# DeltaNet values in a hybrid decoder trunk: convolution along the partitions with shifted copies through DRAM, in place of transposes on TensorE

## The chip, the cores and the metric

The kernel runs on one core of one Trainium2 chip. The metric is the device time of one execution in microseconds (us); the time before is the median of three runs. The profile is one further execution, with its own time. TensorE is called PE (PEld is its weight load), VectorE DVE, ScalarE ACT, GpSimd POOL and SyncE SP. SP computes nothing here; it issues transfers (DMAs), as ACT does too.

## The reference, cut to what matters

There are 256 tokens of width 2048 and two layers. Each layer normalises, projects to 8208 columns, mixes in two branches, projects back, and adds a gated embedding. The change touches the values v of the DeltaNet branch, which has 8 heads of 128:

```
def causal_conv(x, w):      # CONV_WIDTH = 4, one filter per column
    return lax.conv_general_dilated(x, w[:, None, :], (1,), [(CONV_WIDTH - 1, 0)], ...)

def deltanet_branch(qkv, z, b, a, conv_w, A_log, dt_bias, norm_w):
    qkv = jax.nn.silu(causal_conv(qkv, conv_w))
    q, k, v = jnp.split(qkv, 3, axis=-1)
    ...
    o = chunk_gated_delta_rule(q, k, v, g, beta)
    return gated_head_norm(o, z, norm_w)
```

So a value column at token t is silu of the sum over j = 0 to 3 of w[3 - j] times the projected column at token t - j, with zeros ahead of token 0. All is float32.

## The kernel before, in words

The three large products (`in`, `out`, `gate`) run as 392 steps of weights, mostly 512 KB each. For each step SP loads a `raw` tile (`load`, L351), ACT copies it rounded into `whi` (`prep`, L366), DVE makes the remainder `wlo` = raw - whi (L368), and PE multiplies 2 token halves by `whi` and `wlo` (L309): three matmuls for each of two (or four) blocks of 128 rows. There are 3 buffers each of `raw`, `whi` and `wlo`; `ahead` loads up to 4 steps ahead and prepares up to 2 ahead. A step of 12 such matmuls of 512 columns takes some 2.7 us.

The mixers are Python generators that a `tick` after each step advances. A generator yields a count of ticks, out of the tables `DELAY` and `DELAY_AT` (`d2t64`: DeltaNet group 2, step t64), or a condition. A group g has two heads, so 4 groups in 2 layers make 8 instances; `dn12` is layer 1, group 2. Matmuls and transposes go to PE in the order of the program. The other instructions are ordered by a scheduler that works with estimated times, and then each engine runs its own list strictly in that order. SP and ACT issue DMAs the same way: an instruction that waits holds what stands behind it in its own list.

For v (`DN.dv`) the projection comes out of PE with the tokens on the partitions. `evict` (L544) copies it from PSUM to an `et` tile with the row scale, on ACT. After one tick `turned` transposes it on PE (4 transposes of 128x128, `pvc`, L312), so that the columns lie on the partitions and the tokens along a row. `conv` multiplies by the last filter tap on ACT (2 instructions, L607), then adds the other three taps on DVE with slices shifted along the row (6 scalar_tensor_tensor, L611). `sigmoid` takes three ACT and one DVE instructions (L411 to L418), and a DVE product makes silu (L780). After `v` ticks (5; 6 in groups 0 and 3) it is transposed back (4 transposes, `pv`), and DVE scales it by `invn` into `R` (L787). `R` is read much later, when the triangular solve of the group is done.

That solve has a part of its own on DVE, in `q_side` after the wait F: 15 pairs of a product (L701) and a sum (L704) of a small 32-row tile, each needing the one before. It already uses DRAM to rearrange: `d1` is written and read, then `d2`, all issued by ACT.

Buffers that matter: `tmp` has 6 tiles of 128x512, `et` has 2 tiles of 128x1024 shared with the q, k and HGRN2 evictions, and PSUM has 5 banks for the mixers.

Of the kernel before, what the change touches and what calls it, by code (L numbers as in the profile page):

```python
# [16 lines left out]
NG = 4  # L17
# [8 lines left out]
def chunk_cols(chunk):  # L26
# [3 lines left out]


DELAY = {
    "d": {'c': 1, 'D': 4, 'k': 5, 'q': 5, 'ssq': 1, 'F': 3, 'T': 9, 't16': 2, 'p16': 2, 't32': 2, 'p32': 2, 't64': 2, 'p64': 2, 'v': 5, 'z0': 1, 'S': 1, 'w': 1, 'z1': 1, 'o': 1, 'y': 3, 'yp': 1},
    "b": {'o': 1, 'g': 4},
    "h": {'c': 1, 'f': 1, 'a': 4, 'u1': 3, 'u4': 3, 'u16': 3, 'o': 2, 'y': 2, 'yp': 1, 'q': 0},
}

DELAY_AT = {
# [9 lines left out]
}  # L48
# [105 lines left out]


@with_exitstack
def trunk(ctx: ExitStack, tc: tile.TileContext, head, xT, x, pT, W, par, fw, cst, msk, eye, out):
    nc = tc.nc
    pool = lambda name, bufs, **kw: ctx.enter_context(tc.tile_pool(name=name, bufs=bufs, **kw))
    cp = pool("const", 1)  # L160
# [92 lines left out]

    dr = pool("scratch", 1, space=bass.MemoryType.DRAM)
    d2 = dr.tile([66048], F32, name="d2")
    dfull = lambda d: d.rearrange("(i x) -> i x", i=4)[:, 0:16384].rearrange("i (p c) -> p i c", c=128)
    ddiag = lambda d: d.rearrange("(q x) -> q x", q=32)[:, 0:2048].rearrange("q (s f) -> q s f", s=16)[:, :, 0:16]
    SLr = cp.tile([128, 128], F32R, name="SLr")
# [3 lines left out]
    def clear_scratch():  # L262
        V.tensor_copy(SLr, SL)
        G.memset(hA[64:128, :, 0:64], 0.0)
        zero = tp.tile([128, 512], F32, tag="tmp", name="zero")
        G.memset(zero, 0.0)
        tc.keep_in_program_order(nc.scalar.dma_start(out=dfull(d2), in_=zero.rearrange("p (i c) -> p i c", i=4)))

    def P(name, i, n=1):
        o = PAR[name][0] + i  # L270
# [240 lines left out]
    def mix(tag, n, bufs, name):  # L511
        return mp.tile([128, n], F32, tag=tag, name=name, bufs=bufs)

    def v4(ap):
        return ap.rearrange("p (a b) -> p a b", b=128)
# [24 lines left out]
    def evict(ps, c0, n, rt, name):  # L540

        et = mix("et", 1024, 2, name + "et")[:, :2 * n].rearrange("p (t n) -> p t n", t=2)
        for t in range(2):
            S.activation(et[:, t], ps[t][:, c0:c0 + n], AF.Copy, scale=rt[:, t:t + 1])  # L544
        return et

    def turned(et, c0, name):

        ps = pm.tile([128, 512], F32, tag="m", name=name)
        for i in range(4):  # L550
            hh, t = divmod(i, 2)
            PE.transpose(ps[:, 128 * i:128 * i + 128], et[:, t, c0 + 128 * hh:c0 + 128 * hh + 128], ident)
        return ps
# [5 lines left out]
    class DN:  # L559
# [214 lines left out]

        def dv(self, ps, c0):
            n, kq, g = self.n, self.kq, self.g
            et = evict(ps, c0, 256, self.row.rt, n + "v")
            yield self.wait("c")
            ac, sg = self.conv(turned(et, 0, n + "pvc"), 2)
            V.tensor_tensor(ac, ac, sg, ALU.mult)  # L780
            yield self.wait("v")
            yield self.after("k")
            pv = pm.tile([128, 512], F32, tag="m", name=n + "pv")
            for i in range(4):
                PE.transpose(pv[:, 128 * i:128 * i + 128], ac[:, 128 * i:128 * i + 128], ident)
            R = v4(mix("R", 512, 2, n + "R"))
            V.tensor_tensor(R, v4(pv), bc(self.invn, 128), ALU.mult)  # L787
            yield self.after("T")
            yield self.wait("z0")
            v1 = v4(mix("v1", 512, 1, n + "v1"))  # L790

            pz = pm.tile([128, 512], F32, tag="m", name=n + "pz0")
            for hh in range(2):
                PE.matmul(pz[:, 128 * hh:128 * hh + 128], self.Tt[:, 2 * hh], R[:, 2 * hh], start=True, stop=True)
            V.tensor_tensor(v1[:, 0::2], v4(pz)[:, 0:2], bc(self.b[:, 0::2], 128), ALU.mult)
            yield self.wait("S")
            pS = pm.tile([128, 512], F32, tag="m", name=n + "pS")
            for hh in range(2):
                PE.matmul(pS[:, 128 * hh:128 * hh + 128], v4(self.ktail)[:, hh], v1[:, 2 * hh], start=True, stop=True)
            St = v4(mix("St", 256, 1, n + "St"))  # L800
            S.copy(St, v4(pS)[:, 0:2])
            yield self.wait("w")

            pw = pm.tile([128, 512], F32, tag="m", name=n + "pw")
            for hh in range(2):
                for w in range(2):
                    PE.matmul(pw[:, 256 * hh + 128 * w:256 * hh + 128 * w + 128], kq[:, hh, 1, w, :], St[:, hh],
                              start=True, stop=True)
            for hh in range(2):
                V.scalar_tensor_tensor(R[:, 2 * hh + 1], pw[:, 256 * hh:256 * hh + 128], self.neG[:, hh:hh + 1],  # L810
                                       R[:, 2 * hh + 1], ALU.mult, ALU.add)
            qs = v4(mix("qs", 256, 1, n + "qs"))
            V.tensor_tensor(qs, v4(pw)[:, 1::2], bc(self.eG, 128), ALU.mult)
            yield self.wait("z1")
            pz = pm.tile([128, 512], F32, tag="m", name=n + "pz1")
            for hh in range(2):
                PE.matmul(pz[:, 128 * hh:128 * hh + 128], self.Tt[:, 2 * hh + 1], R[:, 2 * hh + 1], start=True, stop=True)
            V.tensor_tensor(v1[:, 1::2], v4(pz)[:, 0:2], bc(self.b[:, 1::2], 128), ALU.mult)
            yield self.wait("o")
            po = pm.tile([128, 512], F32, tag="m", name=n + "po")  # L820
            for i in range(4):
                PE.matmul(po[:, 128 * i:128 * i + 128], self.QK[:, i], v1[:, i], start=True, stop=True)
            o = v4(tmp(n + "o"))
            S.copy(o[:, 0::2], v4(po)[:, 0::2])
            V.tensor_tensor(o[:, 1::2], v4(po)[:, 1::2], qs, ALU.add)
            ss = small("sso")
            for i in range(4):
                S.activation(sp.tile([128, 128], F32, tag="junk", name="junk", bufs=1), o[:, i], AF.Square,
                             scale=self.nq[:, i:i + 1], accum_out=ss[:, i:i + 1])
            f = small("fo")  # L830
            rms_factor(f, ss)
            V.tensor_tensor(f, f, self.nq, ALU.mult)
            yield self.wait("y")
            yield self.after("z")
            yield from head_norm(o, f, self.sz, P("dnw", self.l), g, self.y, n, self.wait("yp"))
# [445 lines left out]
```

## Time and profile before

| | |
|---|---|
| median of three runs (range) | 1279.0 us (1278.23 to 1279.3) |
| the profiled execution: its time / its span | 1276.74 / 1275.0 us |
| granted PE clock, mean | 0.997 |
| PE busy | 1257.1 us (99%) |
| DVE busy | 924.9 us (73%) |
| ACT busy | 782.8 us (61%) |
| POOL busy | 64.0 us (5%) |
| chain that ended last | PE 93%, DVE 5%, issue 1%, ACT 1% |
| DMA | 220.88 MB, SP's queue 51.0% of 16 engines' time, ACT's 2.2% |

The span runs from the first to the last instruction; the profiled execution took 1.74 us more than its span. A busy share says how long an engine had work, not whether it could have done the work faster. Durations of PE overlap: how long a matmul holds PE is read from one start to the next.

### The profile page before, as it was taken

To read this page: it belongs to the slowest core of one execution; us is meant where nothing else is said; L and a number is where in the kernel's file an instruction comes from. 1 tells how busy PE (TensorE), PEld (TensorE's weight loads), DVE (VectorE), ACT (ScalarE), POOL (GpSimd) and SP (SyncE) were. 2 spreads that over 40 slices of the span, in tenths; PEclk is the share of its full clock that TensorE was granted. 3 is DMA by queue.
4 is the path that set the end of the run, shared out by engine and by line. 5 is a ranking of instruction groups with operands and counts; after the bars stand their busy time and mean duration, and the time that the engine had idled before them with its cause. 6 is when DMAs were issued, how large, how long until landed. Compare 5 with 4: busy or idle time off the path is not lost.

```text
span 1275.0 us, 19572 instructions
## 1 busy us (share of the span) xinstructions
PE 1257.1 (99%) x7240; PEld 1044.4 (82%) x7240; DVE 924.9 (73%) x1736; ACT 782.8 (61%) x1400; POOL 64.0 (5%) x55
## 2 busy tenths in 40 slices
PE   8999999999999999999999999999999999999996
PEld 7988887888887888888888888888888888888885
DVE  7789679787796855547668886897777968565575
ACT  7666666666666654437557667667666766444464
POOL 0100010020000000000002000100100000000010
PEclk9999999999999999999999999999999999999998
DMA  8565545445554455555555545544555545555563
GB/s 276 187 226 175 165 153 166 141 158 182 161 173 150 148 172 179 186 187 192 183 186 167 179 163 156 169 145 131 179 180 172 159 149 178 178 182 182 182 198 132
DMA packets 78753, 220.88 MB, mean 173 GB/s; under 512 B 15553, under 2 KB 25281, under 8 KB 78657
## 3 DMA queue, kind: packets, MB, share of 16 engines
q1 hardware_dynamic: 59840, 212.14, 51.0%
q10 hardware_dynamic: 18816, 7.48, 2.2%
q8 instruction: 57, 0.93, 0.3%
q14 instruction: 40, 0.32, 0.1%
HBM read 214.88 MB, written 4.72 MB: 172 GB/s over the span
## 4 chain that ended last, share of the span: by engine, by line
PE 93%; DVE 5%; issue 1%; ACT 1%; DMA 0%; SPq 0%; DVEq 0%; ACTq 0%
PE out L309 14%; PE gate L309 14%; PE in0dk L309 7%; PE in1dk L309 7%; PE in1hf L309 6%; PE in0hf L309 6%; PE in0dv L309 6%; PE in1dv L309 6%; PE in0hi L309 5%; PE in1hi L309 5%; PE up L309 2%; DVE wlo L368 1%; PE in0dz L309 1%; PE in1dz L309 1%; DVE dn12pr L701 0%
## 5 line engine op out<-in xcount | busy, mean ns | idle before, releaser
L368 DVE TENSOR_TENSOR wlo<-raw,whi 128x1024 fp32r<-128x1024 f32 (+1 forms) x394 | 482.4, 1227 | 253.6 <-ACT whi L366 251.6
L366 ACT ACTIVATE whi<-raw 128x1024 fp32r<-128x1024 f32 (+1 forms) x394 | 413.4, 1051 | 356.7 <-PE out L309 88.3
L309 PE MATMUL in1hf<-whi,n1hi 128*128 128x512 f32 x128 | 52.5, 410 | 0.0
L309 PE MATMUL in1hi<-whi,n1hi 128*128 128x512 f32 x128 | 51.6, 403 | 0.0
L309 PE MATMUL in1dk<-whi,n1hi 128*128 128x512 f32 x128 | 51.2, 400 | 0.0
L309 PE MATMUL in1dk<-wlo,n1hi 128*128 128x512 f32 x128 | 50.1, 392 | 0.2 <-DVE wlo L368 0.2
L309 PE MATMUL gate<-whi,g0hi 128*128 128x512 f32 x128 | 50.2, 392 | 0.0
L309 PE MATMUL in1hf<-whi,n1lo 128*128 128x512 f32 x128 | 50.1, 391 | 0.0
L309 PE MATMUL in1hi<-whi,n1lo 128*128 128x512 f32 x128 | 50.0, 391 | 0.0
L309 PE MATMUL in1dk<-whi,n1lo 128*128 128x512 f32 x128 | 50.0, 390 | 0.0
L309 PE MATMUL in1hf<-wlo,n1hi 128*128 128x512 f32 x128 | 49.9, 390 | 0.0
L309 PE MATMUL gate<-whi,g1hi 128*128 128x512 f32 x128 | 49.9, 390 | 0.0
L309 PE MATMUL in1hi<-wlo,n1hi 128*128 128x512 f32 x128 | 49.9, 390 | 0.0
L309 PE MATMUL gate<-whi,g0lo 128*128 128x512 f32 x128 | 49.8, 389 | 0.0
L309 PE MATMUL gate<-wlo,g0hi 128*128 128x512 f32 x128 | 49.8, 389 | 0.0
L309 PE MATMUL gate<-wlo,g1hi 128*128 128x512 f32 x128 | 49.8, 389 | 0.0
L309 PE MATMUL gate<-whi,g1lo 128*128 128x512 f32 x128 | 49.8, 389 | 0.0
L309 PE MATMUL in1dv<-whi,n1hi 128*128 128x512 f32 (+1 forms) x128 | 48.4, 378 | 0.0
L309 PE MATMUL in1dv<-wlo,n1hi 128*128 128x512 f32 (+1 forms) x128 | 46.6, 364 | 0.0
L309 PE MATMUL in1dv<-whi,n1lo 128*128 128x512 f32 (+1 forms) x128 | 46.6, 364 | 0.0
L309 PE MATMUL in0hf<-whi,n0hi 128*128 128x512 f32 x96 | 39.2, 408 | 0.0
L309 PE MATMUL in0hi<-whi,n0hi 128*128 128x512 f32 x96 | 38.5, 401 | 0.0
(1549 smaller groups left out, 3229.0 us busy)
## 6 DMA issues: line engine op xcount, KB each, us to landing
raw<-W SPq DMA_DIRECT2D x384, 512.0 KB, 3.5
raw<-W SPq DMA_DIRECT2D x7, 544.0 KB, 4.1
h<-x SPq DMA_DIRECT2D x4, 512.0 KB, 5.2
xt<-xT SPq DMA_DIRECT2D x3, 512.0 KB, 7.4
out_dram<-h SPq DMA_DIRECT2D x6, 256.0 KB, 2.1
fw<-fw ACTq DMA_DIRECT2D x2, 512.0 KB, 6.0
pin<-pT ACTq DMA_DIRECT2D x2, 256.0 KB, 3.3
out_dram<-h ACTq DMA_DIRECT2D x2, 256.0 KB, 3.0
```

What stands on the lines that cost most here:

```text
L309: return tc.keep_in_program_order(nc.tensor.matmul(*a, **k))
L366: S.activation(hi[:, sl], raw[:, sl], AF.Copy)
L368: V.tensor_tensor(lo[:, sl], raw[:, sl], hi[:, sl].bitcast(F32), ALU.subtract)
```

## The change

The tokens stay on the partitions. `dv` evicts v as before into one half of an `et` tile, and ACT writes it (256 KB) into a DRAM scratch `dsh` behind three rows of zeros. One tick later (`vl`) SP loads the group's filter, repeated on 128 partitions (`cvw`, a new input; 512 KB), and three copies of v, shifted by 1, 2 and 3 tokens (256 KB each). Three ticks later (`vc`) DVE multiplies the four copies by the four rows of the filter and adds them up; the sigmoid follows. After `v` (now 2) ticks four scalar_tensor_tensor write R = conv x invn x sigmoid. Neither `pvc` nor `pv` is transposed any more; the two PSUM banks for them go. At the start two small DMAs on ACT's queue clear the rows of zeros. The delays of a few other steps are changed too.

```diff
-    "d": {... 't64': 2, 'p64': 2, 'v': 5, 'z0': 1, ...},
+    "d": {... 't64': 2, 'p64': 2, 'vl': 1, 'vc': 3, 'v': 2, 'z0': 1, ...},
...
-    "d0D": 6, "d0k": 6, "d0p16": 4, "d0p32": 3, "d0p64": 1, "d0q": 7, "d0t64": 3, "d0v": 6,
+    "d0D": 6, "d0k": 6, "d0p16": 4, "d0p32": 3, "d0p64": 1, "d0q": 7, "d0t64": 3,
...
-    "d2D": 9, "d2k": 3, "d2t64": 4, "d2y": 4, "d2yp": 2, "d2z1": 2,
-    "d3k": 6, "d3o": 2, "d3p64": 3, "d3v": 6, "d3w": 2,
-    "h0a": 5, "h0yp": 2,
-    "h1f": 2, "h1u4": 4, "h1yp": 3,
+    "d2D": 9, "d2k": 3, "d2t16": 1, "d2t64": 6, "d2y": 4, "d2yp": 2,
+    "d3k": 6, "d3o": 2, "d3p64": 3, "d3w": 2,
+    "h0a": 5, "h0u1": 2, "h0yp": 2,
+    "h1f": 2, "h1u4": 4, "h1y": 1, "h1yp": 3,
...
+    dsh = [dr.tile([256 * 259], F32, name=f"dsh{j}") for j in range(2)]
...
+        for d in dsh:
+            tc.keep_in_program_order(nc.scalar.dma_start(out=d[0:768].rearrange("(p f) -> p f", p=128), in_=zero[:, 0:6]))
...
         def dv(self, ps, c0):
             n, kq, g = self.n, self.kq, self.g
-            et = evict(ps, c0, 256, self.row.rt, n + "v")
-            yield self.wait("c")
-            ac, sg = self.conv(turned(et, 0, n + "pvc"), 2)
-            V.tensor_tensor(ac, ac, sg, ALU.mult)
+            full = mix("et", 1024, 2, n + "vet")
+            et, x1 = full[:, :512], full[:, 512:]
+            d = dsh[g % 2]
+            for t in range(2):
+                sl = slice(256 * t, 256 * t + 256)
+                S.activation(et[:, sl], ps[t][:, c0:c0 + 256], AF.Copy, scale=self.row.rt[:, t:t + 1])
+            v2 = lambda ap: ap.rearrange("p (t n) -> p t n", t=2)
+            rows = lambda j: d[256 * (3 - j):256 * (259 - j)].rearrange("(t p n) -> p t n", t=2, p=128)
+            nc.scalar.dma_start(out=rows(0), in_=v2(et))
+            wv = mix("cvw", 1024, 1, n + "cvw")
+            yield self.wait("vl")
+            nc.sync.dma_start(out=wv, in_=cvw[self.l * NG + g])
+            xs = [x1, tmp(n + "vs2"), tmp(n + "vs3")]
+            for j, x in enumerate(xs, 1):
+                nc.sync.dma_start(out=v2(x), in_=rows(j))
+            yield self.wait("vc")
+            w = lambda j: bc1(wv[:, 256 * j:256 * j + 256], 2)
+            V.tensor_tensor(v2(et), v2(et), w(3), ALU.mult)
+            for j, x in enumerate(xs, 1):
+                V.tensor_tensor(v2(x), v2(x), w(3 - j), ALU.mult)
+                V.tensor_tensor(et, et, x, ALU.add)
+            sigmoid(x1, et)
             yield self.wait("v")
             yield self.after("k")
-            pv = pm.tile([128, 512], F32, tag="m", name=n + "pv")
-            for i in range(4):
-                PE.transpose(pv[:, 128 * i:128 * i + 128], ac[:, 128 * i:128 * i + 128], ident)
             R = v4(mix("R", 512, 2, n + "R"))
-            V.tensor_tensor(R, v4(pv), bc(self.invn, 128), ALU.mult)
+            for i in range(4):
+                hh, t = divmod(i, 2)
+                sl = slice(256 * t + 128 * hh, 256 * t + 128 * hh + 128)
+                V.scalar_tensor_tensor(R[:, i], et[:, sl], self.invn[:, i:i + 1], x1[:, sl], ALU.mult, ALU.mult)
             yield self.after("T")
```

## Rows read from the trace of the kernel before

**Rows 1.** The page: span, PE's busy time, and the chain of work that ended last by engine.

```profile
span 1275.0 us, 19572 instructions
PE 1257.1 (99%) x7240; PEld 1044.4 (82%) x7240; DVE 924.9 (73%) x1736; ACT 782.8 (61%) x1400; POOL 64.0 (5%) x55
PE 93%; DVE 5%; issue 1%; ACT 1%; DMA 0%; SPq 0%; DVEq 0%; ACTq 0%
```

**Rows 2.** The waits of PE over the whole span: engine, tile and line <- what it waited for: us in total, times, longest. These are two of the three rows there are; the third repeats the second in the other layer (in1dk).

```profile
PE in0dz L309 <- ACT whi L238: 5.5, 3, 4.4
...
PE in0dk L309 <- DVE wlo L368: 0.2, 1, 0.2
```

**Rows 3.** The timeline of PE around one `pv` group that stands alone: start us, us, what.

```profile
707.53 0.39 PE L309 MATMUL in1hf<-whi,n1lo 128*128 128x512 f32 x1
707.76 0.60 PE L312 MATMUL dn10pv<-cs,dn10vac 128*128 128x128 f32 x4
708.11 0.48 PE L309 MATMUL in1hf<-whi,n1hi 128*128 128x512 f32 x1
708.43 0.40 PE L309 MATMUL in1hf<-wlo,n1hi 128*128 128x512 f32 x1
```

**Rows 4.** The same around a `pvc` group that follows other small matmuls.

```profile
255.18 1.05 PE L309 MATMUL dn01po<-dn01v,dn01QK 128*128 128x128 f32 x8
256.06 0.60 PE L312 MATMUL dn02pvc<-cs,dn02vet 128*128 128x128 f32 x4
256.42 0.47 PE L309 MATMUL in0hi<-whi,n0ahi 128*128 128x512 f32 x1
```

**Rows 5.** The transposes that go, by tile: the first and the last of the 16 groups of 4 (64 in all); duration ns min/median/max, first and last start us.

```profile
L312 PE MATMUL dn00pvc<-cs,dn00vet x4: 272/272/308, 60.0 to 60.4; 128*128 128x128 f32 x4
...
L312 PE MATMUL dn13pv<-cs,dn13vac x4: 273/273/273, 981.9 to 982.2; 128*128 128x128 f32 x4
```

**Rows 6.** The timeline of DVE in layer 0, group 2: start us, us, what. The distance from one start to the next is the time that an instruction holds DVE where it never idles.

```profile
261.60 0.48 DVE L611 SCALAR_TENSOR_TENSOR dn02vac<-dn02pvc,pr,dn02vac 128x254 f32<-128x254 f32 x1
262.00 0.16 DVE L704 TENSOR_REDUCE dn02fx<-dn02pr 32x5 f32<-32x25 f32 x1
...
265.29 1.21 DVE L368 TENSOR_TENSOR wlo<-raw,whi 128x1024 fp32r<-128x1024 f32 x1
...
266.87 0.33 DVE L522 SCALAR_TENSOR_TENSOR dn01yt<-dn01o,fo,dn01sz 128x128 f32<-128x128 f32 x1
267.13 0.26 DVE L701 TENSOR_TENSOR dn02pr<-dn02fx 32x64 f32<-32x64 f32 x1
...
269.73 0.67 DVE L780 TENSOR_TENSOR dn02vac<-dn02vac,dn02vsg 128x512 f32<-128x512 f32 x1
270.33 0.32 DVE L701 TENSOR_TENSOR dn02pr<-dn02fx 32x100 f32<-32x100 f32 x1
...
273.91 0.67 DVE L787 TENSOR_TENSOR dn02R<-dn02pv,invn 128x512 f32<-128x512 f32 x1
...
275.77 1.20 DVE L368 TENSOR_TENSOR wlo<-raw,whi 128x1024 fp32r<-128x1024 f32 x1
```

**Rows 7.** Busy time by stretch: stretch, its length, then busy us (count) of PE, PEld, DVE, ACT, POOL, PE clock, DMA share, GB/s. Group 2 of layer 0, group 2 of layer 1, then groups 3, 1 and 0 of layer 0, around their convolutions.

```profile
256.50:277.00 20.50, 20.37 (x95) 16.61 (x93) 20.05 (x49) 13.67 (x28) 6.29 (x3) 1.00 0.45 153
890.00:905.00 15.00, 15.00 (x71) 12.25 (x69) 14.86 (x36) 8.52 (x12) 4.00 (x1) 1.00 0.42 140
327.00:357.00 30.00, 30.00 (x158) 25.13 (x158) 22.86 (x60) 18.57 (x43) 1.93 (x2) 1.00 0.48 154
137.00:160.00 23.00, 23.00 (x141) 18.40 (x139) 14.42 (x23) 16.07 (x34) 1.28 (x1) 1.00 0.45 151
59.00:83.00 24.00, 24.00 (x117) 19.98 (x116) 20.16 (x41) 16.67 (x40) 3.53 (x3) 1.00 0.66 210
```

**Rows 8.** The timeline of PE behind the convolution of layer 0, group 2; in brackets an idle time ahead of the matmul, and what ended it. 267.65 is the first matmul that reads the remainder of 265.29 in rows 6, and 277.03 the first that reads that of 275.77.

```profile
267.65 0.39 PE L309 MATMUL in0hi<-wlo,n0hi 128*128 128x512 f32 x1
...
276.48 0.39 PE L309 MATMUL in0dk<-whi,n0ahi 128*128 128x512 f32 x1
277.03 0.50 PE L309 MATMUL in0dk<-wlo,n0ahi 128*128 128x512 f32 x1 [0.16 <-DVE wlo L368]
```

**Rows 9.** The timeline of ACT in layer 0, group 2: the second eviction of v, the first of the two tap products, and the rounding of the weights whose remainder is that of 265.29.

```profile
252.31 0.45 ACT L544 ACTIVATE dn02vet<-in0dv,s0rt 128x256 f32<-128x256 f32 x1
...
258.03 0.46 ACT L607 ACTIVATE dn02vac<-dn02pvc,pr 128x256 f32<-128x256 f32 x1
...
262.19 1.06 ACT L366 ACTIVATE whi<-raw 128x1024 fp32r<-128x1024 f32 x1 [0.67 <-PE in0hi L309]
```

**Rows 10.** DMA issues of the whole span: out<-in, queue, count, KB each, median us from issue to landing. The fastest and the slowest write and read of 256 KB in the scratch of the solve stand for their kind.

```profile
raw<-W SPq DMA_DIRECT2D x384, 512.0 KB, 3.5
...
dn00d<-dn00Bt ACTq DMA_DIRECT2D x1, 256.0 KB, 2.3
...
dn03Tt<-d ACTq DMA_DIRECT2D x1, 256.0 KB, 5.4
...
dn12d<-dn12Bt ACTq DMA_DIRECT2D x1, 256.0 KB, 4.1
```

**Rows 11.** The timeline of SP: the issue of the load that the rounding at 262.19 reads.

```profile
255.36 0.33 SPq L351 DMA_DIRECT2D raw<-W  x1
```

More of the change, by code (lines that the diff above doesn't have):

```diff
@@ L32 @@
 DELAY = {
-    "d": {'c': 1, 'D': 4, 'k': 5, 'q': 5, 'ssq': 1, 'F': 3, 'T': 9, 't16': 2, 'p16': 2, 't32': 2, 'p32': 2, 't64': 2, 'p64': 2, 'v': 5, 'z0': 1, 'S': 1, 'w': 1, 'z1': 1, 'o': 1, 'y': 3, 'yp': 1},
+    "d": {'c': 1, 'D': 4, 'k': 5, 'q': 5, 'ssq': 1, 'F': 3, 'T': 9, 't16': 2, 'p16': 2, 't32': 2, 'p32': 2, 't64': 2, 'p64': 2, 'vl': 1, 'vc': 3, 'v': 2, 'z0': 1, 'S': 1, 'w': 1, 'z1': 1, 'o': 1, 'y': 3, 'yp': 1},
     "b": {'o': 1, 'g': 4},
@@ L156, in trunk @@
 @with_exitstack
-def trunk(ctx: ExitStack, tc: tile.TileContext, head, xT, x, pT, W, par, fw, cst, msk, eye, out):
+def trunk(ctx: ExitStack, tc: tile.TileContext, head, xT, x, pT, W, par, cvw, fw, cst, msk, eye, out):
     nc = tc.nc
@@ L776, in dv @@
             n, kq, g = self.n, self.kq, self.g
-            et = evict(ps, c0, 256, self.row.rt, n + "v")
-            yield self.wait("c")
-            ac, sg = self.conv(turned(et, 0, n + "pvc"), 2)
-            V.tensor_tensor(ac, ac, sg, ALU.mult)
+            full = mix("et", 1024, 2, n + "vet")
[20 more added lines that the diff above has]
+            sigmoid(x1, et)
             yield self.wait("v")
             yield self.after("k")
-            pv = pm.tile([128, 512], F32, tag="m", name=n + "pv")
+            R = v4(mix("R", 512, 2, n + "R"))
             for i in range(4):
-                PE.transpose(pv[:, 128 * i:128 * i + 128], ac[:, 128 * i:128 * i + 128], ident)
-            R = v4(mix("R", 512, 2, n + "R"))
-            V.tensor_tensor(R, v4(pv), bc(self.invn, 128), ALU.mult)
+                hh, t = divmod(i, 2)
+                sl = slice(256 * t + 128 * hh, 256 * t + 128 * hh + 128)
+                V.scalar_tensor_tensor(R[:, i], et[:, sl], self.invn[:, i:i + 1], x1[:, sl], ALU.mult, ALU.mult)
             yield self.after("T")
@@ L1269 @@
         "par": np.ascontiguousarray(par),
+        "cvw": np.ascontiguousarray(np.broadcast_to(
+            a["dn_conv_w"][:, :, 2048:].reshape(DEPTH, 4, NG, 256).transpose(0, 2, 1, 3).reshape(DEPTH * NG, 1, 1024),
+            (DEPTH * NG, 128, 1024))),
         "fw": np.ascontiguousarray(np.broadcast_to(a["final_norm_w"], (128, D))), "cst": cst, "msk": msk,
```

## The prediction

> **What bounds the kernel now.** I read the page first: PE is busy 1257.1 of 1275.0 us, and the chain that ended last runs over PE for 93% [rows 1]. A high busy share alone proves little, since PE's durations overlap, so I went to the waits of PE next: outside the start (5.5 us) PE waits 0.2 us per layer in all, each time for a weight remainder of DVE [rows 2]. So PE is fed without a gap, and whatever leaves its list shortens the run by the time from one start to the next, as long as nothing else becomes late. The second question is therefore how far DVE, ACT and SP are from being late. The busy times by stretch answer it: around the convolution of group 2, DVE is busy 20.05 of 20.50 us in layer 0 and 14.86 of 15.00 in layer 1, against 22.86 of 30, 14.42 of 23 and 20.16 of 24 us in groups 3, 1 and 0 [rows 7]. Both of PE's 0.2 us waits lie at the end of those full stretches; the first is seen at 277.03 [rows 8]. There the margin is nothing. This is the place that decides.
>
> **PE: what goes.** Sixteen groups of four transposes leave, 64 instructions [rows 5]. A group that stands alone: from 707.53 to 708.43 are 0.90 us, of which two ordinary matmuls take 0.23 each (707.53 to 707.76), so the group costs 0.44 us; part of that is the slow first matmul behind it (708.11 to 708.43, 0.32) [rows 3]. A group behind other small matmuls costs 256.42 - 256.06 = 0.36 us, because the slow matmul stays [rows 4]. In the timeline five groups stand alone and eleven do not: 5 x 0.44 + 11 x 0.36 = 6.2 us. Bounds: 5.8 if none stood alone (16 x 0.36), 7.0 if all did. Nothing covers this work, so the whole is on the path.
>
> A transpose lasts 272 ns in the trace [rows 5] although four of them occupy 0.36 us [rows 4]. [...]
>
> **DVE: what is exchanged.** Where DVE never idles, one start to the next gives: a tap 0.40 us (261.60 to 262.00), a product of 512 columns 0.60 (269.73 to 270.33), a scalar_tensor_tensor of 128 columns 0.26 (266.87 to 267.13) [rows 6]. Before: 6 taps, silu product, R (as long as the silu product) = 2.40 + 0.60 + 0.60 = 3.60 us. After: four products and three sums of 512, and four of 128 = 7 x 0.60 + 4 x 0.26 = 5.24 us; the sigmoid's own instruction stays. So DVE gains 1.64 us of work per instance, 13.1 us in all. In groups 0, 1 and 3 DVE idles 3.8 to 8.6 us in the stretch [rows 7], which hides 1.64; I cost it at nothing there, and with the cover gone it is at most 1.64 each.
>
> In group 2 there is no cover. The remainder begun at 275.77 is the one for which PE waits at 277.03 [rows 6, 8]. After the change PE arrives there 2 x 0.36 = 0.72 us earlier, since both transposes of the group lie ahead. What DVE has ahead of that remainder changes too: if all of the convolution stays ahead of it, DVE is 1.64 us later and PE stalls 0.72 + 1.64 = 2.4 us. But the convolution now starts 4 ticks after the chunk instead of 1, and behind its sums come three ACT steps of the sigmoid and the two ticks of `v`; so R (1.04 us) will, I think, fall behind the remainder, where before it stood ahead (273.91). Then DVE's load ahead of it is 4.20 in place of 3.60, 0.6 us more, and the stall 1.3 us. It could be nothing if the scheduler, which knows the load, draws the remainder forward. I take 1.3 (bounds 0 and 2.4), twice: 2.6 us. The next remainder then has PE later and DVE free again, so nothing adds.
>
> **ACT and the queues.** ACT loses two instructions of 0.46 us (258.03) per instance, and gains one DMA issue; an issue takes 0.33 us on SP [rows 9, 11]. It gains more than it pays, and waits only for its own eviction just before. The two clearing DMAs at the start (0.7 us of ACT by that price) have the same source and wait as the one ahead of them; the weights there are two steps ahead, so nothing. SP gains four issues per instance (1.3 us): the filter, then three reads that wait for ACT's write. Behind them in SP's list stand the weight loads, and behind those ACT, DVE and PE. The eviction ends at 252.31 + 0.45 = 252.76 [rows 9]; a write of 256 KB to the scratch lands 2.3 to 4.1 us after its issue [rows 10], at 255.1 to 256.9, and the reads are up one tick (2.7 us) after the chunk. So SP stands still for at most 1.5 us past 255.36, where it next issues a load [rows 11]. That load lands by the median 3.5 us later [rows 10], at 258.9, and ACT takes it at 262.19 [rows 9]: 3.3 us of slack; its remainder ends at 265.29 + 1.21 = 266.50 and PE reads it at 267.65 [rows 6, 8]: 1.15 more. Some 4.4 us cover 1.5 + 1.3, so I cost SP's wait at nothing; the price without cover stands under the last rival but one. The reads (a read of 256 KB landed 5.4 us after its issue at the slowest [rows 10]) have three ticks, 8 us, before DVE asks for them; were they late, DVE would stand still with weight remainders behind it, which belongs to that rival.
>
> [...]
>
> Held buffers: `et` is now kept for some six ticks, but the next eviction into that pair comes eight steps later, and the `tmp` tiles stay two. Five PSUM banks serve fewer users: a gain that I put at nothing, as PE waits for none [rows 2]. The changed delays of steps in d2, h0 and h1 move small matmuls together or apart, 0.09 us each (0.32 - 0.23, the slow matmul behind a group [rows 3]); both signs, nothing.
>
> **Sum.** 1276.74 (the profiled execution) - 6.2 + 2.6 = 1273.1. The median of the runs stands 2.3 above the profiled execution, so 1275.4.
>
> **The rivals.**
> - *The whole gain stays.* The scheduler draws the remainders of group 2 ahead of the convolution. For it: the filters come later in the program than the weights of four steps. Against it: the remainder was the last thing DVE finished in time. 1279.0 - 6.2 = 1272.8; with more groups alone, 1272.0.
> - *DVE is the bound of more than one place.* Group 2 costs 2.4 us per layer: 1279.0 - 6.2 + 4.8 = 1277.6. If groups 0 and 3, where DVE is 84% and 76% busy [rows 7], also give their own 0.72 back (four instances, 2.9), 1280.5. I call it 1278.9: no change.
> - *SP's queue jams.* The four transfers stand ahead of the weights: the wait of 0 to 1.5 us, 1.3 of issues, and 1.31 MB ahead in the same queue. At 0.45 of the DMA time 153 GB/s are moved [rows 7], so 340 at full share, and 3.9 us for those bytes. The weights come 5.2 to 6.7 us late against 4.4 of slack: 0.8 to 2.3 us per instance. With 1.5 on each of eight, 1272.8 + 12 = 1285. From 1.1 us per instance it is slower than before. For it: SP's list is strict. Against it: SP runs up to three loads ahead, and in groups 0, 1 and 3 DVE has room to catch up.
> - *A transpose costs its duration.* 64 x 0.272 = 17.4 us: 1261.6. Rows 4 speak against it.
>
> **How the numbers follow.** This measurement can tell about 0.2% (2.6 us) from no change: faster is below 1276.4, slower above 1281.6. Chances: my forecast 0.37 (own range 1273.6 to 1277.0), whole gain 0.30, DVE 0.18, SP 0.13, duration 0.02. Faster: 0.27 of the first, 0.30, 0.01 and 0.02, together 0.60. Same: 0.10, 0.14 of DVE and 0.02 of SP, 0.26. Slower: 0.03 of DVE and 0.11 of SP, 0.14. The range 1271.8 to 1281.0 leaves out the duration case, most of SP's and the edges, some 0.17.
>
> **What would show it.** L312 has 64 PE instructions fewer and no `pvc` or `pv`. DVE's busy time rises by about 13 us, ACT's falls by about 7. PE waits for `wlo` once per layer, over 1 us, behind group 2's convolution, and hardly elsewhere. Were there no such wait, the whole gain stays; were there waits of `whi` for DMA, or of the convolution for its copies, SP's rival. A time over 1277.6 with PE waiting nowhere would contradict the reading that PE's list is the path.

## The result, and the profile after

The changed kernel takes 1282.14 us (median of 19 runs, 1279.45 to 1286.34); the kernel before, beside it, 1278.23 (1276.77 to 1279.39). The ratio is 1.0032, 95% interval 1.0025 to 1.0040: some 4 us slower. The prediction was 1275.4, with 1281.0 as the upper end of its range: wrong in sign, and outside. The profiled execution took 1281.01 us, its span is 1279.2.

The page after, the lines that answer to [rows 1]:

```profile
span 1279.2 us, 19485 instructions
PE 1254.9 (98%) x7176; PEld 1039.7 (81%) x7176; DVE 938.0 (73%) x1760; ACT 778.3 (61%) x1384; POOL 63.9 (5%) x55
PE 81%; DVE 9%; ACT 4%; DMA 4%; issue 2%; SPq 0%; ACTq 0%; DVEq 0%
```

PE has its 64 instructions fewer, DVE 13.1 us more; both are what was forecast. The last line tells the rest: of the chain that ended last, PE holds 81% where it held 93%. DVE, ACT and DMA have got into it. Where, the waits of PE tell (columns as in [rows 2]):

```profile
PE in0dz L313 <- ACT whi L238: 6.0, 3, 4.5
PE in0dk L313 <- DVE wlo L372: 2.8, 1, 2.8
PE in0hi L313 <- DVE wlo L372: 0.9, 1, 0.9
PE in1hf L313 <- DVE wlo L372: 0.8, 1, 0.8
PE in0dk L313 <- ACT hg00fqet L548: 0.7, 1, 0.7
PE in1dk L313 <- DVE wlo L372: 0.5, 1, 0.5
PE dn12pp L313 <- DVE dn12T L715: 0.2, 1, 0.2
```

One wait stands out, 2.8 us in layer 0. To price the stretches I lined up the two traces by the weight loads (392 steps, in the same order in both) and took, for each stretch, by how much the start of the first matmul behind it moves from its beginning to its end (times are counted from the first matmul of each trace). In us, minus is a gain; a group's stretch is from its projection to that of the next one, and `start` is what lies ahead of the first group:

```
                        start  L0g0  L0g1  L0g2+3  L1g0  L1g1  L1g2+3   all
changed kernel           1.70  5.05 -0.91   -0.36 -0.24 -0.65   -0.27  4.33
forecast                 0    -0.78 -0.78   -0.25 -0.78 -0.78   -0.25  -3.6
```

(The forecast row: 6.2/8 per instance, and 1.3 of stall in group 2 of each layer.) Five columns bear the prediction out within 0.6 us. Two don't. The start differs from execution to execution, as two kernels below show whose instructions on every engine stand in the same order for the first 280 us: -0.04 and 1.70. It goes with the moment at which the granted clock of PE becomes 1.00: 11.59 us in the trace before and 14.64 in the changed kernel. A matmul of 272 columns lasts 0.43 us ahead of that moment and 0.29 behind it (11.14 and 11.73 before); in the first of these two kernels it lasts 0.29 at 11.88, in the second still 0.43 at 11.83. So I do not count the start to the change, and the loss is one column: group 0 of layer 0, 5.8 us from its forecast.

**How it comes about.** The wait itself, in the timeline of PE:

```profile
100.02 0.39 PE L313 MATMUL in0dk<-whi,n0lo 128*128 128x512 f32 x1
100.25 0.39 PE L313 MATMUL in0dk<-whi,n0hi 128*128 128x512 f32 x1
103.45 0.80 PE L313 MATMUL in0dk<-wlo,n0hi 128*128 128x512 f32 x1 [2.81 <-DVE wlo L372]
104.04 0.63 PE L313 MATMUL in0dk<-whi,n0lo 128*128 128x512 f32 x1
```

Behind it the matmuls start 0.43 us apart (104.04 to 104.47 is the next) and not 0.23. The stretches say why (columns as in [rows 7]; the number behind POOL is PE's clock):

```profile
97.00:100.00 3.00, 3.00 (x15) 2.50 (x15) 3.00 (x9) 2.84 (x4) 0.00 (x0) 1.00 0.75 237
103.40:106.80 3.40, 3.35 (x8) 2.67 (x9) 3.40 (x7) 1.02 (x3) 0.00 (x0) 0.50 0.68 237
```

The granted clock falls to 0.50 from 103.38 for 3.41 us, which is 1.7 us lost on top of the 2.8. With the 0.7 us for which PE waited for `hg00fqet` (near 86 us), that makes 5.2 of the 5.8.

The remainder that PE waits for is late because it stands in DVE's list behind the scans of `hg00`, and those behind the solve of DeltaNet's group 0, on a DVE that is full there (11.90 of the 12 us from 92 to 104). DVE's timeline before, and then after:

```profile
95.60 1.25 DVE L876 TENSOR_TENSOR_SCAN hg00G<-cs,hg00fsg 128x256 f32<-128x256 f32 x2
96.78 1.19 DVE L368 TENSOR_TENSOR wlo<-raw,whi 128x1024 fp32r<-128x1024 f32 x1
```

```profile
99.25 0.67 DVE L901 TENSOR_TENSOR_SCAN hg00G<-cs,hg00fsg 128x256 f32<-128x256 f32 x1
...
100.91 0.35 DVE L708 TENSOR_REDUCE dn00fx<-dn00pr 32x15 f32<-32x225 f32 x1
...
102.19 1.20 DVE L372 TENSOR_TENSOR wlo<-raw,whi 128x1024 fp32r<-128x1024 f32 x1
```

Before, this remainder ended at 97.97 and PE read it at 98.21: 0.24 us of margin, with 12.00 of 12 us busy on DVE from 92 to 104. After, it ends at 103.4. So what made the solve late? One looks for its first input, the products `Bt`, and for what stands ahead of them. Before, then after:

```profile
70.84 0.61 DVE L678 SCALAR_TENSOR_TENSOR dn00Bt<-dn00pg,nb,dn00Dt 128x128 f32<-128x128 f32 x2
```

```profile
69.92 2.13 DVE L802 TENSOR_TENSOR dn00vs<-dn00vs,dn00cvw 128x512 f32<-128x512 f32 x2
73.03 1.23 DVE L372 TENSOR_TENSOR wlo<-raw,whi 128x1024 fp32r<-128x1024 f32 x1 [0.98 <-ACT whi L370]
...
74.57 0.69 DVE L803 TENSOR_TENSOR dn00vet<-dn00vet,dn00vs 128x512 f32<-128x512 f32 x1
...
75.60 1.23 DVE L372 TENSOR_TENSOR wlo<-raw,whi 128x1024 fp32r<-128x1024 f32 x1 [0.26 <-ACT whi L370]
...
77.69 0.61 DVE L682 SCALAR_TENSOR_TENSOR dn00Bt<-dn00pg,nb,dn00Dt 128x128 f32<-128x128 f32 x2
```

`Bt` comes 6.9 us later, 5.1 of it beyond the start. Two things stand ahead of it now: products and sums of the copies, and remainders that wait for weights while `Bt` could have run. The weights are late because SP's list holds the three reads right behind an early weight load: the next weight load is issued at 66.14, where before the same load was issued at 60.71. The waits of SP for the write, the longest, that of this group, and the shortest of the eight:

```profile
SPq L797 <- DMA dsh<-dn02vet: 6.3, 1, 6.3
...
SPq L797 <- DMA dsh<-dn00vet: 5.4, 1, 5.4
...
SPq L797 <- DMA dsh<-dn10vet: 0.8, 1, 0.8
```

Then the solve's own way through DRAM grows: from the issue of `Bt`'s write to that of the read back, before and after:

```profile
72.32 0.39 ACTq L685 DMA_DIRECT2D dn00d<-dn00Bt  x1
74.65 0.33 ACTq L689 DMA_DIRECT2D dn00fx<-dn00d  x1
```

```profile
79.17 0.39 ACTq L689 DMA_DIRECT2D dn00d<-dn00Bt  x1
83.05 0.33 ACTq L693 DMA_DIRECT2D dn00fx<-dn00d  x1
```

3.9 us in place of 2.3. It falls into this stretch of DMA (72 to 83 us, before and after; the last two columns are DMA share and GB/s):

```profile
72.00:83.00 11.00, 11.00 (x54) 9.04 (x53) 7.80 (x15) 5.99 (x16) 1.02 (x1) 1.00 0.69 218
```

```profile
72.00:83.00 11.00, 10.87 (x50) 8.65 (x49) 9.60 (x23) 7.63 (x19) 0.75 (x1) 1.00 0.85 296
```

There the filter of group 1 (issued at 74.66), the weights that SP held back and a residual load (77.23; four of 512 KB in all, only in layer 0) come together; the three reads of group 0 have landed by 68.7. That its transfers make the round trip longer is not shown: in two kernels below it is 4.6 us without them, and 2.3 us with them and the old convolution. Before, the read back landed at 77.6 and the solve began at 82.0, so there were 4.4 us of slack; after, 86.1 and 86.6. The slack is spent, and the margin of 0.24 us behind it with it.

That is a reading of one trace. The runs below take it apart.

### The profile page after: what moved, and what is told of

Its sections match the earlier page's. It is cut to its first block, busy times and chain, and to the rows that moved or that the text cites. A ratio compares the mean times of both kernels' runs of the same rounds, so it can differ in the third digit from the quotient of the medians.

```text
span 1279.2 us, 19485 instructions
## 1 busy us (share of the span) xinstructions
PE 1254.9 (98%) x7176; PEld 1039.7 (81%) x7176; DVE 938.0 (73%) x1760; ACT 778.3 (61%) x1384; POOL 63.9 (5%) x55
## 4 chain that ended last, share of the span: by engine, by line
PE 81%; DVE 9%; ACT 4%; DMA 4%; issue 2%; SPq 0%; ACTq 0%; DVEq 0%
PE out L313 14%; PE gate L313 14%; PE in1dv L313 5%; PE in0dv L313 5%; PE in0hi L313 5%; PE in1hi L313 5%; PE in0dk L313 5%; PE in1dk L313 5%; PE in0hf L313 5%; PE in1hf L313 4%; DVE wlo L372 3%; PE up L313 2%; ACT whi L370 1%; PE in0dz L313 1%; DMA raw<-W 1%
## 5 line engine op out<-in xcount | busy, mean ns | idle before, releaser
L313 PE MATMUL in0dk<-wlo,n0hi 128*128 128x512 f32 x96 | 38.3, 399 | 2.8 <-DVE wlo L372 2.8
```

Source lines behind the costliest of these rows:

```text
L313: return tc.keep_in_program_order(nc.tensor.matmul(*a, **k))
```

## The experiments

Medians of five rounds against the kernel before (1277.7 to 1277.9 in all these batches). Kernels of different batches are compared by their ratios.

**Is PE the path?** The changed kernel with the transposes back, as dummy work: `turn_again("pvc")` ahead of the copies and `turn_again("pv")` ahead of `R`, each four transposes of `et` that nobody reads.

> The changed kernel with the 64 transposes back as work that nobody reads (4 of v ahead of the reads, 4 ahead of R, each group into a PSUM bank). If PE's list is the path everywhere, 6.2 us more, 1288. If the weights are late at the places of the stalls, these transposes fall into the stalls there and it is 3 to 5 us more, 1285 to 1287. If PE were not the bound, no more than 1283.

Measured: 1289.89 us, ratio 1.0098 (1.0083 to 1.0112); 0.0066 over the changed kernel, 8.4 us. That is more than the 6.2 us that the prediction took; the edit has opened a wait of its own too (`dn12pp`, 1.3 us, in place of 0.2). In group 1, where nothing stalls in either kernel, the lined-up traces put the price of two groups of transposes at 0.90 and 0.68 us in the two layers, against 0.78 forecast. The gain is real; something takes away more than it.

**The delays.** The kernel before with only the delays of other steps changed:

```diff
-    ... "d2t64": 4, ... "d2z1": 2, ...
+    ... "d2t16": 1, "d2t64": 6, ... "h0u1": 2, ... "h1y": 1, ...
```

> The kernel before with only the changed delays of the other steps (d2t16, d2t64, d2z1, h0u1, h1y); its convolution is untouched. Queue theory (the copies' reads wait in SP's list and make the weights late) and DVE theory (1.64 us more DVE work per instance makes the weight remainders late): 1278 us, as before, within 1. Delay theory (the moved steps cost the 4 us): 1281 or more.

Measured: 1285.05 us, ratio 1.0061 (1.0049 to 1.0073). Its two longest waits of PE behind the start show that the loss is at another place than that of the changed kernel:

```profile
PE dn12pp L309 <- DVE dn12T L711: 2.3, 1, 2.3
PE dn02pp L309 <- DVE dn02T L711: 1.9, 1, 1.9
```

The solve of group 2 is finished too late for its product on PE, in both layers. The changed kernel has this wait with 0.2 us only, so the delays go with the new convolution of group 2. They are not its loss; two runs further down come back to this.

**Is it SP's wait?** First the three reads from another, cleared scratch (`rows` takes `dsr` for j > 0), so that nothing waits for the write. Then SP's loads kept in the order of the program, with three ticks ahead of the reads (`keep_in_program_order` on weights, filter and reads, `'vl': 3`).

> The changed kernel, but the three shifted copies are read from another scratch that is zero from the start, so that the reads wait for no write of ACT; the same bytes move and DVE does the same work (the values then hold only the token's own tap). Queue theory: SP's waits of 4 to 6 us go, the 3 us stall of PE in layer 0, group 0 goes, 1275 to 1277 us. DVE theory: PE still waits for remainders there, 1281 to 1283.

> The changed kernel with SP's loads kept in the order of the program and the filter and the copies read 3 ticks after the chunk instead of 1, so that they stand two weight loads later in SP's list; all results as before. Queue theory: SP hardly waits for the write any more, 1275 to 1278 us. DVE theory: 1281 or more, since DVE's work is the same.

Measured: 1287.67 us, ratio 1.0077 (1.0062 to 1.0092), and 1296.30, ratio 1.0149 (1.0131 to 1.0167). Both slower; the stall near 100 us is still there (2.4 and 3.1 us), and new ones have come (in the first, `dn02ssk` and `dn12ssk` wait 1.6 us each for `kq`). The times speak against SP's wait as the whole cause; but both edits turned the lists over at many places (DVE's order differs from the changed kernel's at 147 and 175 places), so they decide nothing.

**Bytes, or DVE's work?** Four runs: the residual loads moved from the weight loads 22, 25, 28, 31 to 52, 56, 60, 64; the filter loaded once (`wv = filt`, 3.5 MB less); the third copy's product and sum left out (`if j < 3`, 1.2 us of DVE less per instance by the distances of starts, 7.5 us less busy time in all by the page); and the kernel before with the write and the three reads into places that nobody uses.

> The changed kernel with the four 512 KB loads of the residual h, which nothing reads before the out stage, moved from weight loads 22 to 31 to weight loads 52 to 64, away from group 0's solve in layer 0. Transfer theory (in layer 0 the solve's round trip through DRAM is slowed by the new transfers on top of the residual's, the solve ends late and holds DVE, PE stalls 3 us near 100 us and its clock is halved for 3.4 us): that stall shrinks to the 0.7 us of layer 1, 1276 to 1278. DVE theory (1.64 us more DVE work per instance is the cause): the stall stays above 2 us, 1281 to 1283.

> The changed kernel with one filter tile loaded once near the start, which all eight instances use (so seven of them use the filter of layer 0, group 0): 3.5 MB of loads on SP's queue fewer, all else as in the changed kernel. Transfer theory: 1278 to 1281, a part of the 4 us comes back. DVE theory: 1281 to 1283.

> The changed kernel with the product and the sum of the third shifted copy left out (the tap at t - 3 is missing from the values); the copy is still read. DVE has 1.2 us less per instance, so nearly the work of the kernel before. DVE theory: the stalls shrink to a fraction, 1275 to 1278. Transfer theory: 1280 to 1282.

> The kernel before with the write of v to the scratch and the three shifted reads added (1 MB per instance, no filter), into places that nobody uses; its transposes and its convolution stay. Transfer theory: slower than before, 1281 to 1286, with the stall near 100 us in layer 0. DVE theory: 1278, as before.

Measured, in this order: 1279.98 (1.0021, 1.0013 to 1.0030), 1281.33 (1.0022, 1.0012 to 1.0031), 1283.00 (1.0039, 1.0027 to 1.0051), 1281.28 (1.0026, 1.0018 to 1.0035). Moving or leaving out loads helps by some 1.4 us each, about what the intervals can tell; the time with less DVE work is no lower. That speaks against the plain DVE theory (13 us more work, so later everywhere). But the stall near 100 stays in the first three (2.9, 3.7, 1.8 us), and the transfers alone, in the kernel before, cost 0.2 us in that stretch. The stretch itself says more than the medians: layer 0's group 0 costs 3.8 us with the residual loads moved and 3.0 with two copies, in place of 5.05, so both count there, and other places take the gain back. No single one of the four removes the loss; the next runs ask where it sits.

**Where?** The old convolution in group 0 of both layers, the new one in groups 1 to 3; the same with the residual loads moved; and the old one in group 0 of layer 0 alone (`g == 0 and self.l == 0`).

```diff
+            if g == 0:
+                et = evict(ps, c0, 256, self.row.rt, n + "v")
...
+                V.tensor_tensor(R, v4(pv), bc(self.invn, 128), ALU.mult)
+            else:
```

> The changed kernel with the old convolution (transposes, taps out of PSUM, v at 6 ticks in group 0) in group 0 of both layers; groups 1 to 3 keep the new one. Two of eight instances give back their two groups of transposes, 2 x 0.77 = 1.5 us. Order theory (in group 0 the new convolution stands ahead of the Bt products in DVE's list, so the solve starts late, runs into the scans of HGRN2 and makes PE wait near 100 us; 2.8 us and the half clock behind it, 4.6 in all): no gap over 0.6 us between 95 and 105 us, Bt at 71 to 73 us, 1278 to 1279.5 us. Reshuffle theory (every edit of the list opens stalls of 1 to 3 us somewhere, that place is only one of many): the gap near 100 may go, others come, 1281 to 1285.

> The kernel with the old convolution in group 0, and the four residual loads moved from raw loads 22 to 31 to 52 to 64. Transfer theory: another 1 to 2 us less than the kernel with the old convolution in group 0 alone, 1276 to 1278. Order theory alone: the same as that one, since nothing is late any more in that stretch, 1278 to 1279.5. Reshuffle theory: 1281 to 1285.

> The changed kernel with the old convolution in group 0 of the first layer only; the second layer's group 0 has the new one. If the loss of group 0 needs what only the first layer has (the residual loads among the weights of that stretch), the second layer's group gains its 0.8 us: 1273.5 to 1275 beside 1275.1 for the kernel with the old convolution in both. If both layers' group 0 lose alike (some 3 us each), 1277.5 to 1279.5.

Measured: 1275.13 us (ratio 0.9980, 0.9971 to 0.9989), 1277.31 (0.9999, 0.9990 to 1.0008), 1276.46 (0.9989, 0.9980 to 0.9997). The first is below the kernel before, and 0.0052, 6.6 us, below the changed kernel, although it gives back two instances' transposes. Its waits of PE, but for one of 0.2 us:

```profile
PE in0dz L313 <- ACT whi L238: 5.2, 2, 4.5
PE dn12pp L313 <- DVE dn12T L715: 1.2, 1, 1.2
PE in1hf L313 <- DVE wlo L372: 0.5, 1, 0.5
```

No wait near 100, `Bt` at 70.8 and the solve's products from 82.0 to 94.8, to a tenth as before the change. It is lower than any theory had it, since the loss in group 0 was more than the one wait and its clock. With nothing late there, moving the residual loads gains nothing; it costs 0.0019, as another turn of the lists can. Layer 1's group 0 alone gains 0.80 us in the lined-up traces (0.78 forecast), and layer 0's alone was the loss; in the medians that kernel is 0.0009 above the first, which its interval can't tell from 0 or from 2 us, so whether layer 1's group pays over many runs stays open.

**The work or the transfers of group 0?** The changed kernel without the write, the filter and the reads in group 0 (`if g:` ahead of each of them; the products take `et` and a constant tile); and the kernel with the old convolution in group 0, with the four transfers added there, unused.

> The changed kernel without the write, the filter load and the three reads in group 0 of both layers; the products there take the evicted values and a constant tile in place of copies and filter (their sums are subtractions), so that DVE's instructions in group 0 are as many and as large as in the changed kernel, but no copy is shifted: group 0's values are not computed. Transfer theory (the four transfers of group 0 make its solve and its weights late): no gap over 1 us near 100 us and near 730 us, 1274 to 1276. DVE theory (the 1.64 us more of group 0 in a stretch whose margin is 0.24 us): the gap near 100 stays over 2 us, 1280 to 1283. Both together: the gap 1 to 2 us, 1277 to 1279.

> The kernel with the old convolution in group 0 (1275.1), and in group 0 of both layers also the new one's write, filter load and three reads into places that nobody uses. Transfer theory: Bt, the solve and the weight remainders of group 0 come late as in the changed kernel, a gap over 1.5 us near 100 us, 1279 to 1282. DVE theory: within 1 us of the kernel without the transfers, 1275 to 1276.

Measured: 1275.91 us (0.9985, 0.9976 to 0.9993) and 1277.80 (0.9997, 0.9988 to 1.0006). The longest waits of PE behind the start, of the first and of the second:

```profile
PE dn00pg L313 <- DVE dn00kq L623: 1.1, 1, 1.1
PE in0dk L313 <- DVE wlo L372: 1.0, 1, 1.0
PE dn02pp L313 <- DVE dn02T L715: 0.9, 1, 0.9
```

```profile
PE in0hf L313 <- DVE wlo L372: 1.7, 1, 1.7
PE in1hf L313 <- DVE wlo L372: 0.9, 1, 0.9
PE in0dk L313 <- DVE wlo L372: 0.7, 1, 0.7
```

Against the kernel with the old group 0 (0.9980), the DVE work alone costs 0.0005 and hides 1.5 us of gain: 2.1 us. The transfers alone cost 0.0017: 2.2 us. Both together cost 0.0052 and hide the same 1.5: 8.1 us. That is nearly 4 more than the sum; the ratios leave some 2 us of doubt in it. The lined-up traces (table below) put nearly none of it into the place of the loss: in layer 0's group 0 the work alone costs 1.59 + 0.78 = 2.4 us, the transfers alone 2.95 + 0.14 = 3.1, and both 5.05 + 0.78 = 5.8, against a sum of 5.5 (0.7 us more in the transfers' `start`, a wait for `dn00kqet`, is not in it). So that both together cost more than their sum is not shown. Each alone makes waits of 1 to 2 us, and the mean granted clock is 0.997 as before the change; together they make one of 2.8, and the clock falls too (0.50 for 3.41 us, mean 0.995). By its time the first run speaks for the transfers, while the second falls between the two theories; with the stretches, it is both, in parts of like size.

The transfers alone also make `Bt` late, by 4.1 us beyond the start, though the work ahead of it is the old one. DVE stands still for a rounded weight:

```profile
74.19 1.23 DVE L372 TENSOR_TENSOR wlo<-raw,whi 128x1024 fp32r<-128x1024 f32 x1 [4.80 <-ACT whi L370]
...
77.54 0.61 DVE L682 SCALAR_TENSOR_TENSOR dn00Bt<-dn00pg,nb,dn00Dt 128x128 f32<-128x128 f32 x2
```

The work alone makes `Bt` 2.2 us late, and both 5.1. How much a wait of SP costs depends on the lists around it: in the kernel before with the write and the reads added, SP waits as long (5.2 us), and the stretch loses 0.2. Why so little there is open.

**Is it the order ahead of Bt?** Five ticks in place of one ahead of the reads in group 0 (`"d0vl": 5`), which puts two of the three copies behind `Bt` in DVE's list (DVE's order differs at 45 places in all); and this with the residual loads moved. The edit moves transfers too: two of the three reads are issued at 72.0 and 72.5 in place of 64.3 and 65.6, and the weight load that stood behind them at 63.72 in place of 66.14.

> The changed kernel with 5 ticks in place of 1 ahead of the reads in group 0 of both layers, so that two of the three copies are multiplied and added behind the Bt products (some 2.4 us of DVE work move behind them); all else is as in the changed kernel, all 64 transposes stay away, all bytes stay. Order theory: Bt comes 2 us earlier or more, the gap near 100 us shrinks from 2.8 to under 1 us and the half clock there goes, 1277 to 1279. Transfer theory (Bt and the weights are late by the transfers, not by the list): the gap stays over 2 us, 1281 to 1283. Reshuffle theory: 1281 to 1285 with stalls elsewhere.

> The changed kernel with both: 5 ticks ahead of the reads in group 0, and the residual loads moved to raw loads 52 to 64. If order and transfers together make the whole loss, the gap near 100 us is under 0.6 us and the time 1275 to 1277, below the kernel before. If the order is all of it, 1277 to 1279 as without the move. If the transfers are all of it, 1279 to 1281 as with the residual loads moved alone. Reshuffle theory: 1281 to 1285.

Measured: 1280.09 us (1.0018, 1.0008 to 1.0027) and 1282.01 (1.0036, 1.0024 to 1.0049). In the first, `Bt` comes at 72.7, 0.3 us later than before the change if one takes off the start, and the stretch of layer 0's group 0 costs 1.1 us in place of 5.05; the wait near 100 us shrinks from 2.8 to 1.8, not under 1 as the order theory had it. Less the 0.78 of the forecast, 1.8 is 1.0 of those 1.1 us, so by this estimate no clock is lost there. So what stands ahead of `Bt` is most of the loss; but since weights come earlier as well, the run doesn't part the order on DVE from the wait of SP. The time is above the order theory's range, for the delay holds for both layers, and layer 1 now has a wait of its own:

```profile
PE in1dk L313 <- DVE wlo L372: 2.6, 1, 2.6
PE in0dk L313 <- DVE wlo L372: 1.8, 1, 1.8
```

Layer 1's group 0 goes from -0.24 to +2.07. With the residual loads moved as well, `Bt` is at 76.6 again and the wait 2.8: the scheduler had put the copies ahead of it once more. The delay in layer 0 alone was not tried.

**Group 2, and the delays once more.** The old convolution in groups 0 and 2; the same again with five ticks of `v` in group 2; and the kernel with the old group 0 with the delays of the other steps as they were before.

> The new convolution in groups 1 and 3 alone, the old one in groups 0 and 2 of both layers. Against the kernel with the old one in group 0 alone (1275.1): two more instances give back 1.5 us. If group 2 has no cover on DVE, as the prediction had it (a stall of 1.3 us per layer), the stalls near 275, 287 and 913 us go and the time is 1274 to 1275, the lowest. If group 2 is paid for in full, 1276.5 to 1277.

> The kernel with the new convolution in groups 1 and 3 alone, once more, with the 5 ticks of v that group 2 had before; with 2 ticks its transposes stood in PE's list ahead of their convolution and PE waited 7.0 us in each layer, which was a fault of the edit. Against the kernel with the old convolution in group 0 alone (1275.1): two more instances give back 1.5 us. If group 2 has no cover on DVE, as the prediction had it (1.3 us per layer), the stalls near 275, 287 and 913 us go: 1274 to 1275.2. If group 2 gains in full, 1276.5 to 1277.5.

> The kernel with the old convolution in group 0, and the delays of the other steps (t16, t64 and z1 of DeltaNet's group 2, u1 and y of HGRN2's groups 0 and 1) as in the kernel before. Theory that these delays are what made the old kernel 6 us slower when they alone were changed, by a late dn02T and dn12T: the waits of dn12pp near 913 go, 1272 to 1274. Theory that they fit the new convolution and only it: 1277 to 1280.

Measured: 1292.26 us (1.0107, 1.0094 to 1.0121), 1279.87 (1.0017, 1.0009 to 1.0026) and 1275.98 (0.9984, 0.9975 to 0.9992). The first tells nothing of group 2 (7.0 us of wait per layer for `vac`, since `pv` was scheduled with the new, short delay). The second doesn't tell what it was made for either, for the old convolution meets the changed delays again:

```profile
PE dn12pp L313 <- DVE dn12T L715: 2.2, 1, 2.2
PE dn02pp L313 <- DVE dn02T L715: 1.8, 1, 1.8
```

The same two waits as with the delays alone. The third run lies between its two theories: with the new convolution in group 2 the changed delays are worth nothing that can be measured (0.9980 and 0.9984), while with the old one they cost. What group 2's stall costs can be read from the lined-up traces only.

The stretches of the runs that decide, against the kernel before:

```
                        start  L0g0  L0g1  L0g2+3  L1g0  L1g1  L1g2+3   all
changed kernel           1.70  5.05 -0.91   -0.36 -0.24 -0.65   -0.27  4.33
old conv in g0          -0.04 -0.14 -0.90   -1.07 -0.11 -0.86    0.47 -2.65
old conv in dn00         1.70 -0.14 -0.86    0.05 -0.80 -0.89    0.32 -0.62
g0: work, no transfers   2.00  1.59 -0.91   -0.48 -0.75 -0.48   -0.84  0.13
g0: transfers, old work  2.58  2.95 -0.91   -1.13 -0.11 -0.91   -0.14  2.33
g0: copies behind Bt     1.62  1.09 -0.90   -1.32  2.07 -0.83   -0.06  1.66
```

## Why the prediction was wrong

- *PE, 6.2 us off the path.* Right. Group 1's two columns, where nothing stalls, are -0.91 and -0.65 against -0.78; the transposes put back cost 8.4, and 0.90 and 0.68 in group 1. The rival by which a transpose costs its duration (17.4 us) is out.
- *DVE 1.64 us more per instance.* Right: 13.1 us in all, on the page. ACT's busy time falls by 4.5 us and not by 7; nothing hangs on it.
- *Group 2 pays 1.3 us per layer.* Right in sum, and partly by luck: groups 2 and 3 together -0.36 and -0.27 against -0.25, but in the five other kernels of the last table, with the same convolution in these groups, the two columns run from -1.32 to 0.47. In layer 0 the wait is where it was expected (`in0hi`, 0.9 us, not over 1); in layer 1 another stands for it (`in1hf`, 0.8).
- *"In groups 0, 1 and 3 DVE idles 3.8 to 8.6 us in the stretch [...], which hides 1.64; I cost it at nothing there."* This step failed, in one instance of six. For group 0 I had the stretch 59 to 83 us, 20.16 of 24 us busy [rows 7]. Cut at `Bt`, the same trace says 12.36 of 13.00 us busy from 59 to 72 and 7.80 of 11.00 behind. The idle time was behind the products that the solve starts from, the new work came ahead of them. Cost in layer 0 with the transfers beside it: 5.8 us; the work alone 2.4 there, and 2.1 in both layers by the medians.
- *"I cost SP's wait at nothing."* This step failed at the same place. The wait was mis-sized: up to 1.5 us forecast, 4.4 to 6.3 us measured in seven of eight. I had taken it that a read is up one tick after the chunk; the tick only ranks the instructions, and the scheduler set the reads right behind an early weight load, ahead of the write's landing. In groups 1 to 3 it still cost nothing that the columns show, although the waits there (4.4 to 6.3 us) use up the 4.4 us of slack that I had counted; why is open. In layer 0's group 0 the transfers alone cost 3.1 us. SP's rows show a read's wait keeping what stands behind it in the list: 5.4 us for the write there, and the next weight load issued at 66.14 in place of 60.71. My rival of the jammed queue (1285 us) named this mechanism, but priced it at 1.5 us in each of eight; it is one place, and DVE's work has a like part in it.
- *"Both signs, nothing"* for the delays. Wrong as a rule (1.0061 in the old kernel), right as it was used here (0.9980 and 0.9984 with and without).
- *Not in the prediction at all:* that a late solve has 4.4 us of slack and then a margin of 0.24 us, and that a wait of PE can be followed by half its clock (2.81 us, then 0.50 for 3.41 us).

The median stands 3.9 us above before; the lined-up stretches without the start give 2.6. The rest isn't placed: the runs of the changed kernel spread over 6.9 us (before: 2.6), so its waits are probably not the same from one to the next, and I have one trace of it.

## What to carry to other kernels

Cover is not idle time per stretch: cut the stretch at the first product that a long chain starts from, and ask whether the new work comes ahead of it or behind. Where an engine's list is strict, a weight conversion that waits for its load holds back the chain behind it, so added transfers can make an engine late that has no more work than before: with the transfers of group 0 alone, DVE stood 4.80 us ahead of a remainder, and `Bt` behind it came 4.1 us late beyond the start. And such a rewrite need not be taken whole: in six of its eight instances it is a gain of 0.2%, 1275.13 us, the lowest median of this study.

## What the hardware showed that was not expected

The clock record of the changed kernel is 1.00 from 14.64 to 103.38 us, 0.50 for 3.413 us, and 1.00 again up to 1270.74: the two stretches of 1.00 (88.75 and 1163.94 us) are 26.0 and 341.0 times the length of that fall. Before, it is 1.00 from 11.59 to 1267.70 without a fall between, 368.0 times that length. The fall came behind a wait of 2.81 us; waits of 0.9 us and less in the same trace brought none. With the delays alone, a wait of 1.89 us ahead of the small matmuls of `dn02pp` (64x32, at 291.57) stands ahead of a clock of 0.50 from 292.30 to 295.60. In the kernel with the copies behind `Bt`, waits of 1.8 and 2.6 us between large matmuls lie in stretches that end 1.87 and 2.85 us above their forecast (1.09 and 2.07, each plus 0.78), which by my estimate leaves no room for 1.7 us of halved clock. So the length of a wait alone doesn't say in these runs whether the clock falls, and what does is not shown. A wait of 1.8 to 2.8 us cost its length, or 1.7 us more; that may be part of why runs of a kernel with such waits spread more (6.9 us, before 2.6).

And where a run's first rise falls moves its time too: in the changed kernel the matmuls of 512 columns start 0.43 us apart ahead of it (13.26, 13.69, 14.11) and 0.23 behind (14.82, 15.05), and it comes at 14.64 us in place of 11.59. Half of these 3.05 us, 1.5, is my estimate of what that costs, most of the 1.70 in the `start` column.
